# Two layers with recurrent mixers on one core: the second part of 59 weight units by an accumulating transfer within SBUF

## The chip, the cores and the metric

The kernel runs on one core of a Trainium2 chip. The metric is the device time of one launch in microseconds (us). TensorE (PE) multiplies, VectorE (DVE), ScalarE (ACT) and GpSimd (POOL) work on elements, and transfers are issued from the queue of SyncE (SP) or of POOL and are carried out by 16 DMA engines. PE keeps a queue for loading weights of its own (PEld).

## The reference

A prompt of 512 tokens and 8 samples of one token each go through two layers of width 1024. The first layer joins a gated linear recurrence (RG-LRU) and a state-space scan (SSD), the second is a gated linear attention with 16 heads (HGRN2). Each layer ends with a gated embedding. All is float32.

```python
def layer_ab(h, p, ...):
    u = rmsnorm(h, norm_w) @ w_in
    a_x, a_gate, b_z, b_xbc, b_dt = jnp.split(u, ...)
    ...                                   # convolutions, RG-LRU, SSD
    mix = jnp.concatenate([a_out, b_out], axis=-1).astype(h.dtype) @ w_out
    h = h + mix
    h = per_layer_embed(h, p, ple_w, ple_g)

def layer_c(h, p, ...):
    u = rmsnorm(h, norm_w) @ w_in
    q, fx, v, gate = jnp.split(u, [HK_C, 2 * HK_C, 2 * HK_C + D_C], axis=-1)
    ...                                   # chunks of 128 tokens, 16 heads
    h = h + o.astype(h.dtype) @ w_out
    h = per_layer_embed(h, p, ple_w, ple_g)

def per_layer_embed(h, p, w_proj, w_gate):
    gate = jax.nn.sigmoid((h @ w_gate).astype(F32))
    return h + (gate * (p @ w_proj).astype(F32)).astype(h.dtype)
```

## The kernel before

Tokens lie along the free axis (520 = 512 + 8), features on partitions. A projection is computed in tiles of 128 output features. For float32 accuracy each weight and each activation is split into two parts of type float32r (`hi`, the rounded value, and `lo`, the rest), and three of the four products are added: `whi` by `xh`, `whi` by `xl`, `wlo` by `xh`, each for two halves of 260 tokens. A *unit* is a block of weights of 128 partitions x 1024 elements (512 KB), mostly 8 blocks of 128 rows by 128 columns; it makes 48 products.

Units are read in program order: `ax` (the recurrence's input), `xbc` (12 units), `z` and `ag` (gates, 8 units each), `oa` and `ob` (output), `pg` (the embedding's gate), and in layer 1 for each pair of heads two units each of `f`, `v`, `q`, `g`, and at times four of the output `o`. `section` lists them in *groups* of two neighbouring units, which `load_group` brings in by one transfer of 1 MB on SP's queue into one of two buffers `wraw` (128 x 2048). `split_unit` copies a unit to `whi` (on ACT or DVE) and subtracts: `wlo` = `wraw` - `whi` on DVE. Two buffers each of `whi` and `wlo` feed PE.

```python
            copy(hv, v)
            tt(lv, v, hv.bitcast(F32), SUB, eng)
```

All instructions are first recorded by `Plan` and then put in an order: with an estimate of each cost, an engine that comes free takes the recorded instruction of the earliest place in the program whose operands are there. `side(...)` moves the place of what is recorded in it; `SPLIT_AHEAD` and `LOAD_AHEAD` say how many us of the main stream ahead of a unit its splitting and its loading stand. The order found so is fixed: each engine and each queue runs its own list in order and waits at the first entry that is not ready. All instructions are issued by one line (L510), so the profile is read by the names of tiles.

Beside the projections stand: the small products on POOL that make `dtt` (the step sizes of the SSD, through `htmp`), on which the product `acs` of PE waits; `wsl`, the SSD's weights; `smp`, the samples' states of the SSD (512 KB in and out); `l1c` and `l1d`, the same in layer 1; `pl`, the embedding, kept in DRAM (`pl_d`) until its gate is there.

Of the kernel before, what the change touches and what calls it, by code (L numbers as in the profile page):

```python
# [42 lines left out]
# how far ahead of a unit its weights are split and loaded, in us of the main stream  # L43
SPLIT_AHEAD, LOAD_AHEAD = 1.67, 11.54
# how far ahead of the main stream goes what it waits for, in us
MARGIN = 38.78
# an engine waits for an instruction that is more urgent by URGENT us, up to this part of the time of the one at hand
# [32 lines left out]
def _mm(n, a, k):  # L80
    out, m = k["out"] if "out" in k else a[0], k["lhsT"].shape[-1]
    if m < 128 and out.off >= 32 * ROW:
        # beside the one before it, in other columns of the array
        return 65 if k["rhs"].dtype == F32R else 125
    return max(n, 256) if k["rhs"].dtype == F32R else 4 * max(n, m)
# [17 lines left out]
class Buf:  # L103
    """A tile that is allocated when its first instruction is issued."""
# [7 lines left out]
class View:  # L112
    """A view of a Buf; offset and strides are in elements, a partition is ROW apart."""
# [86 lines left out]
class Op:  # L200
    """One instruction, in a form for each engine that may take it, or a few matrix products that stay together."""
# [8 lines left out]
class Plan:  # L210
    """Instructions are collected first and then put in an order: with an estimate of what each of them costs, an
    engine that comes free takes the instruction of the earliest place in the program whose operands are there."""
# [6 lines left out]
    # -- collecting --  # L219
# [22 lines left out]
    @contextmanager  # L242
    def side(self, start=0.0, rate=0.0, pinned=False):
        """Instructions whose place is moved, by a start and by their own time so far; pinned: for good."""
        keep = self.shift, self.rate, self.pinned
        self.shift, self.rate, self.pinned = start, rate, pinned
        yield
        self.shift, self.rate, self.pinned = keep

    @contextmanager  # L250
    def together(self, *views):
        """Instructions that wait until all of some operands are written."""
        self.gate = self.barrier([o for v in views for box, o, w in v.buf.acc if w and _meet(box, v.box())])
        yield
        self.gate = None

    @contextmanager
    def block(self, main=False):
        """Matrix products that stay together."""
# [66 lines left out]
    # -- ordering --  # L326
    def hold_banks(self):
        """A PSUM bank is taken only when what its readers wait for otherwise is already on its way."""
# [7 lines left out]
    def urgency(self):  # L336
        """What an instruction of the main stream waits for is put ahead of it."""
# [10 lines left out]
    def order(self):  # L348
# [44 lines left out]
        def pick(e, t):  # L393
            """The instruction for engine e at time t, or when there may be one."""
# [7 lines left out]
            while av:  # L402
# [13 lines left out]
                if func and table not in IN_SET[func]:  # L416
                    # another table: first what the loaded one can do, for a while
# [14 lines left out]
            if got:  # L432
                heapq.heappush(av, got)
                hold = {"dve": HOLD_DVE, "act": HOLD_ACT, "pool": HOLD_POOL}.get(e)
                if hold:
                    # rather wait a little for one that is more urgent than be in its way
# [8 lines left out]
        while left:  # L445
# [27 lines left out]
            else:  # L473
                if e == "pe":
                    # the clock is halved after a window with too few columns
# [17 lines left out]
    # -- issuing --  # L493
# [27 lines left out]
# the place of the side work: its start after the instructions it follows, and its pace  # L521
# [9 lines left out]
def hybrid_decode_step_kernel(ctx: ExitStack, tc: tile.TileContext, I, O, mode="both"):  # L531
# [31 lines left out]
    def grab(name):  # L563
        """One of four PSUM banks for the side work; it is given back by its last reader."""
        return new("psa", [128, 512], "ax", name)
# [25 lines left out]
    def copy(out, in_):  # L591
        """A copy on either engine."""
        plans[-1].record(("act", "copy", (out, in_), {}), ("dve", "tensor_copy", (out, in_), {}))

    def scaled(out, in_, s):
        """in_ times a column, on either engine."""
# [10 lines left out]
    groups, units, sec = [], [], {}  # L607

    def section(name, ap, k0, kk, c0, ncols, uc, per=2):
        sec[name] = len(units)  # L610
        for c in range(c0, c0 + ncols, per * uc):
            w = min(per * uc, c0 + ncols - c)
            groups.append((ap, k0, kk, c, w))
            for s in range(0, w, uc):
                units.append((len(groups) - 1, s, uc, kk))

    raw_of, split_of = {}, {}

    def load_group(g):
        ap, k0, kk, c, w = groups[g]  # L620
        r = new("wp", [128, 2048], "raw", f"wraw{g}", 2)
        v = r[:, :kk * w].rearrange("p (k c) -> p k c", k=kk)
        with side(*((plans[-1].shift, 0.0, True) if plans[-1].pinned else (-LOAD_AHEAD,))):
            sp.dma_start(out=v, in_=ap[k0 * 128:(k0 + kk) * 128, c:c + w].rearrange("(k p) c -> p k c", p=128))
        raw_of[g] = v

    def split_unit(u, hi=None, lo=None, eng=dve):
        g, s, uc, kk = units[u]
        if g not in raw_of:
            load_group(g)  # L630
        v = raw_of[g][:, :, s:s + uc]
        if hi is None:
            hi = new("wp", [128, 1024], "whi", f"whi{u}", 2, F32R)
            lo = new("wp", [128, 1024], "wlo", f"wlo{u}", 2, F32R)
        hv = hi[:, :kk * uc].rearrange("p (k c) -> p k c", k=kk)
        lv = lo[:, :kk * uc].rearrange("p (k c) -> p k c", k=kk)
        with side(*((plans[-1].shift, 0.0, True) if plans[-1].pinned else (-SPLIT_AHEAD,))):
            copy(hv, v)
            tt(lv, v, hv.bitcast(F32), SUB, eng)
# [5 lines left out]
    section("ax", w_in0, 0, 8, 0, 256, 128, 1)  # L645
    section("ax2", w_in0, 0, 8, 256, 768, 128)
    section("proj0", I["ple_proj"][0], 0, 2, 0, 512, 256, 1)
    section("proj0b", I["ple_proj"][0], 0, 2, 512, 512, 512, 1)
# [30 lines left out]
    pair_sections("r", "fgvq")  # L679
    K8 = list(range(8))  # L680

    def project_both(tiles, pair, kmap):
        """One or two tiles of 128 output features (column block m of unit u) over all tokens."""
# [28 lines left out]
    def split_p(pk, ps8, pp, layer):  # L712
        """p with features on partitions, in two float32r parts."""
# [23 lines left out]
    for i in range(2):  # L737
        with side(-69.0, pinned=True):
            load_group(units[sec["proj0"] + i][0])
        with side(-67.0 + i * W1, pinned=True):  # L740
            split_unit(sec["proj0"] + i)
    with side(-65.0, pinned=True):
        for i in range(4):
            if i == 1:
                load_group(units[sec["proj0b"]][0])
# [17 lines left out]
    # the tensor engine's clock rises only under load: products of constants until the first tokens are there  # L763
# [43 lines left out]
    def rsqrt_mean(dst, src, n, width):  # L807
        """(src / n + eps) ** -0.5 on a few columns."""
# [8 lines left out]
    def scale_split(src, w, R, xh, xl, name):  # L817
        """src times its weight and a row of factors per token, in two float32r parts."""
# [6 lines left out]
    # the tokens with features on partitions; they come back as the residual  # L825
# [94 lines left out]
    def log1p_of(z, n, lo):  # L920
        """log(1+z) for z in [0,1], from the odd series in z/(2+z)."""
# [14 lines left out]
    def accurate_exp(t, k):  # L936
        """exp in place: the table on x/2^k, where it is exact to float32, and k squarings."""
# [4 lines left out]
    def buffers():  # L942
        """Samples: convolution buffers and LRU state with features on partitions."""
# [11 lines left out]
    def tables():  # L955
        pool.memset(triu, 1.0)
        select(triu, [[1, 128]], 0, -1, 0.0)
        # RG-LRU: -8 softplus(-lam), halved for the sigmoid from tanh
# [10 lines left out]
        # the convolution on x/B/C is halved: silu(2 y) = y (1 + tanh(y))  # L969
# [9 lines left out]
    def lower_bounds():  # L979
        """The lower bound of layer 1 is the second of two softmax rows."""  # L980
# [10 lines left out]
        # is every lower bound large enough for one reference per chunk of layer 1?  # L991
# [6 lines left out]
        # if not, the fast way runs on bounds that keep it finite, and its results are replaced  # L998
# [5 lines left out]
        # with sigmoid(x) = (1 + t) / 2, t = tanh(x / 2): k = cneg (t - 1), decay = ch t + fb  # L1004
# [10 lines left out]
    # the first weights have a place of their own  # L1015
# [41 lines left out]
    def gates(j):  # L1057
        """r and i as tanh of the halved argument; 1 - a^2 = (1 + a^2) tanh(-log a)."""
# [37 lines left out]
    def lru(j0):  # L1096
        """The recurrence over the prompt and one step of the samples."""
# [70 lines left out]
    def dt_project():  # L1168
        """dt with heads on partitions, the parts of its weights side by side, then with tokens there; the fifth
        block ends with the samples."""  # L1170
# [85 lines left out]
    def ssd_chunk(g, c):  # L1256
# [11 lines left out]
        # exp(acs_t - acs_s) for s <= t  # L1268
# [17 lines left out]
        # features on partitions: two heads side by side  # L1286
# [44 lines left out]
    def smp_start(g):  # L1331
        """B and C of the samples on every partition, by way of DRAM."""
# [771 lines left out]
```

## Time and profile before

| | before |
|---|---|
| time, median of 3 runs | 1078.1 us (1075.42 to 1078.21) |
| span of the profiled execution | 1075.0 us |
| its own time | not listed apart; the three runs are 0.4 to 3.2 us above the span |
| busy PE, DVE, ACT, POOL | 1044.0, 778.2, 509.1, 144.6 us |
| bytes moved by DMA | 138.43 MB, 129 GB/s over the span |

The page gives busy time by engine, then groups of instructions (name of the output, names of the inputs, partitions x elements, count, busy us, mean ns of one, idle time of the engine before them and what ended it). A wait names the waiting instruction first, then what released it. A row of a stretch gives start and end, the stretch's length, the busy time of each engine, the granted clock of PE, the mean busy share of the 16 DMA engines and GB/s.

### The profile page before, as it was taken

How to read it: one execution, taken by the hardware profiler on the slowest of the kernel's cores; microseconds unless marked ns; L12 is line 12 of the kernel's file. 1: busy time of each engine (PE TensorE's matmuls, PEld its weight loads, DVE VectorE, ACT ScalarE, POOL GpSimd, SP SyncE). 2: the span in 40 equal slices, each digit the busy share in tenths (PEclk: the TensorE clock that was granted, in tenths of full speed). 3: DMA queues.
4: the chain of work that ended last, by engine and by line, in shares of the span. 5: the costliest groups of instructions: out<-in, count | busy, mean ns of one | idle time of the engine just before them, and what ended most of it. 6: DMA issues, size and time to landing. Idle time of an engine off the chain costs nothing.

```text
span 1075.0 us, 21235 instructions
## 1 busy us (share of the span) xinstructions
PE 1044.0 (97%) x8595; PEld 1023.0 (95%) x8595; DVE 778.2 (72%) x1521; ACT 509.1 (47%) x1196; POOL 144.6 (13%) x247
## 2 busy tenths in 40 slices
PE   9899989999999999999999999999999999999995
PEld 8899988899999999999999999999999999999995
DVE  6879988999997546774858576675765757667753
ACT  6476648636464212353445545333463344642453
POOL 3755475200000000100000000000000000000000
PEclk9899999999999999999999999999999999999998
DMA  8603226444686233563433433253342433335311
GB/s 275 244 21 99 80 51 206 147 142 140 200 249 210 79 115 131 162 208 88 135 108 115 128 102 111 90 155 91 115 124 87 143 98 112 97 89 199 119 40 44
DMA packets 130466, 138.43 MB, mean 129 GB/s; under 512 B 13704, under 2 KB 111128, under 8 KB 130344
## 3 DMA queue, kind: packets, MB, share of 16 engines
q1 hardware_dynamic: 130136, 136.93, 41.0%
q8 instruction: 69, 1.13, 0.4%
q14 instruction: 37, 0.30, 0.1%
q0 software_dynamic: 224, 0.06, 0.0%
HBM read 111.71 MB, written 25.44 MB: 128 GB/s over the span
## 4 chain that ended last, share of the span: by engine, by line
PE 84%; POOL 5%; DVE 4%; DMA 3%; ACT 2%; issue 1%; POOLq 0%; ACTq 0%; DVEq 0%
PE o L510 11%; PE g L510 10%; PE f L510 9%; PE v L510 9%; PE q L510 9%; PE pg L510 7%; PE ag L510 4%; PE ob L510 4%; PE z L510 4%; PE oa L510 3%; PE ax L510 3%; PE xbc L510 1%; POOL csm L510 1%; PE A L510 1%; PE kv L510 1%
## 5 line engine op out<-in xcount | busy, mean ns | idle before, releaser
L510 DVE TENSOR_TENSOR wlo<-wraw,whi 128x1024 fp32r<-128x1024 f32 (+1 forms) x143 | 173.4, 1213 | 3.2 <-ACT whi L510 1.8
L510 ACT CAST whi<-wraw 128x1024 fp32r<-128x1024 f32 (+1 forms) x63 | 65.2, 1036 | 126.3 <-PE q L510 41.2
L510 POOL TENSOR_TENSOR at__1873<-at__1873,nhalf 128x4 f32<-128x4 f32 (+1 forms) x24 | 20.8, 866 | 501.1 <-DVE at__1873 L510 501.1
L510 DVE CAST whi<-wraw 128x1024 fp32r<-128x1024 f32 x80 | 55.3, 692 | 36.7 <-PE v L510 11.9
L510 PE MATMUL g<-xh,whi 128*128 128x260 f32 x256 | 55.8, 299 | 0.0
L510 PE MATMUL q<-xh,whi 128*128 128x260 f32 x256 | 53.2, 289 | 0.0
L510 PE MATMUL o<-oh,whi 128*128 128x260 f32 x256 | 52.6, 286 | 0.0
L510 PE MATMUL v<-xh,whi 128*128 128x260 f32 x256 | 52.1, 285 | 0.0
L510 PE MATMUL v<-xh,wlo 128*128 128x260 f32 x256 | 51.5, 283 | 0.0
L510 PE MATMUL g<-xl,whi 128*128 128x260 f32 x256 | 51.5, 283 | 0.0
L510 PE MATMUL o<-oh,wlo 128*128 128x260 f32 x256 | 51.5, 283 | 0.0
L510 PE MATMUL g<-xh,wlo 128*128 128x260 f32 x256 | 51.5, 283 | 0.0
L510 PE MATMUL o<-ol,whi 128*128 128x260 f32 x256 | 51.4, 282 | 0.0
L510 PE MATMUL q<-xl,whi 128*128 128x260 f32 x256 | 51.4, 282 | 0.0
L510 PE MATMUL v<-xl,whi 128*128 128x260 f32 x256 | 51.4, 282 | 0.0
L510 PE MATMUL q<-xh,wlo 128*128 128x260 f32 x256 | 51.4, 282 | 0.0
L510 PE MATMUL f<-xh,whi 128*128 128x260 f32 x240 | 50.6, 292 | 0.0
L510 PE MATMUL f<-xl,whi 128*128 128x260 f32 x240 | 48.2, 282 | 0.0
L510 PE MATMUL f<-xh,wlo 128*128 128x260 f32 x240 | 48.2, 282 | 0.0
L510 DVE SCALAR_TENSOR_TENSOR l1a<-q,lbt,l1a 128x260 f32<-128x260 f32 (+1 forms) x32 | 14.0, 479 | 44.1 <-PE q L510 44.0
L510 DVE SCALAR_TENSOR_TENSOR l1c<-l1d,l1c 128x128 f32<-128x128 f32 x128 | 40.9, 345 | 0.6 <-ACT l1c L510 0.6
L510 PEld LDWEIGHTS o<-oh,whi 128*128 128x128 f32 x256 | 39.3, 189 | 0.9 <-issue 0.8
(507 smaller groups left out, 3362.2 us busy)
## 6 DMA issues: line engine op xcount, KB each, us to landing
wraw<-in_c_w_in_dram SPq DMA_DIRECT2D x32, 1024.0 KB
wraw<-in_ab_w_in_dram SPq DMA_DIRECT2D x15, 1024.0 KB
wraw<-in_ab_w_out_dram SPq DMA_DIRECT2D x8, 1024.0 KB
wraw<-in_ple_gate_dram SPq DMA_DIRECT2D x8, 1024.0 KB
l1c<-in_state_c_dram SPq DMA_DIRECT2D x16, 512.0 KB
out_dram<-l1c SPq DMA_DIRECT2D x16, 512.0 KB
wraw<-in_c_w_out_dram SPq DMA_DIRECT2D x8, 1024.0 KB
pl<-pl_d SPq DMA_DIRECT2D x2, 2080.0 KB
```

Source lines behind the costliest of these rows:

```text
L510: getattr(f, name)(*a, **k)
```

## The change

Units are loaded one at a time, 512 KB each, into two buffers `wraw` of half the size; the space goes to a third buffer each of `whi` and `wlo`. For the units in `by_dma` (the 28 of `xbc`, `z` and `ag`, and in layer 1 the second unit of each `f`, `v`, `q`, `g`, except the first pair's `f`: 31) the second part is made otherwise: `whi` is copied, `wlo` is set to its negative on ACT or DVE, and a transfer issued by POOL adds `wraw` to `wlo` (both in SBUF, 128 rows of 4 KB). These three stand `HI_AHEAD` = 11.0 us ahead, loads 15.0 instead of 11.54. The embedding `pl` is read back in eight pieces instead of one transfer, in both layers. Comments are dropped; all other constants stay.

```diff
-SPLIT_AHEAD, LOAD_AHEAD = 1.67, 11.54
+SPLIT_AHEAD, LOAD_AHEAD, HI_AHEAD = 1.67, 15.0, 11.0
...
-def load_group(g):
-        ap, k0, kk, c, w = groups[g]
-        r = new("wp", [128, 2048], "raw", f"wraw{g}", 2)
...
+    def wtile(tag, u, bufs, dt=F32R):
+        _, kk, uc = units[u]
+        return new("wp", [128, 1024], tag, f"{tag}{u}", bufs, dt)[:, :kk * uc].rearrange("p (k c) -> p k c", k=kk)
...
+    def load_raw(u):
+        raw_of[u] = wtile("wraw", u, 2, F32)
+        with ahead(LOAD_AHEAD):
+            sp.dma_start(out=raw_of[u], in_=units[u][0])
...
-        with side(*((plans[-1].shift, 0.0, True) if plans[-1].pinned else (-SPLIT_AHEAD,))):
-            copy(hv, v)
-            tt(lv, v, hv.bitcast(F32), SUB, eng)
+        rv = raw_of[u]
+        if u not in by_dma:
+            with ahead(SPLIT_AHEAD):
+                copy(hv, rv)
+                tt(lv, rv, hv.bitcast(F32), SUB, eng)
+        else:
+            with ahead(HI_AHEAD):
+                copy(hv, rv)
+                scaled(lv, hv.bitcast(F32), -1.0)
+                pool.dma_start(out=lv, in_=rv, accum_op=ADD)
...
+    by_dma.update(range(sec["xbc"], sec["out0a"]))
+    by_dma.update(sec[f"{nm}{pr}"] + 1 for nm in "fvqg" for pr in range(8) if nm + str(pr) != "f0")
...
-    sp.dma_start(out=pl0, in_=pl_d[0].rearrange("k p n -> p k n"))
+    for j in range(8):
+        with side(2.67 * j):
+            sp.dma_start(out=pl0[:, j], in_=pl_d[0][j])
...
-        with side(-20.0):
-            sp.dma_start(out=pl1, in_=pl_d[1].rearrange("k p n -> p k n"))
+        for j in range(8):
+            with side(-12.0 + 2.67 * j):
+                sp.dma_start(out=pl1[:, j], in_=pl_d[1][j])
```

How the lists change at the places of which the prediction speaks. First SP's queue late in layer 0, where PE works on `ag` and then on the last four `z`; before it reads:

```order
L510 DMA wraw_3042<-in_ab_w_in_dram 128x8x256
L510 DMA smp<-in_state_b_ssm_dram 128x8x128
L510 DMA out_dram<-wsl 128x4x128
L510 DMA wraw_3226<-in_ab_w_in_dram 128x8x256
L510 DMA out_dram<-smp 128x8x128
L510 DMA smp<-in_state_b_ssm_dram 128x8x128
```

and of the changed kernel:

```order
L510 DMA wraw_3083<-in_ab_w_in_dram 128x8x128
L510 DMA out_dram<-smp 128x8x128
L510 DMA out_dram<-wsl 128x4x128
L510 DMA wraw_3206<-in_ab_w_in_dram 128x8x128
L510 DMA smp<-in_state_b_ssm_dram 128x8x128
L510 DMA out_dram<-smp 128x8x128
L510 DMA wraw_3295<-in_ab_w_in_dram 128x8x128
```

Loads have half the columns and stand twice as often between the states; each waits for the buffer of the unit two before it.

Second POOL's list in `xbc`, where `dtt` is made through `htmp` (`xa` and `LCb` belong to the recurrence and the convolution). Before:

```order
L510 TENSOR_SCALAR dtt<-dtt 128x80
L510 TENSOR_SCALAR htmp<-dtt 128x80
L510 TENSOR_TENSOR xa<-lr,AH_507 128x8
L510 TENSOR_TENSOR htmp<-dtt,htmp 128x80
L510 COPY LCb<-bcs 128x11
```

and of the changed kernel:

```order
L510 COPY LCb<-bcs 128x11
L510 TENSOR_SCALAR dtt<-dtt 128x80
L510 DMA wlo_1669<-wraw_1544 128x1024
L510 TENSOR_SCALAR htmp<-dtt 128x80
L510 TENSOR_TENSOR htmp<-dtt,htmp 128x80
```

The issue of an accumulating transfer stands between two steps of the chain; two more follow further down, ahead of its end. On PE the product `acs`, which waits for this chain, stands 12 products later in `xbc` than before.

Third ACT's list late in layer 0, where `sga` is the first step on a finished unit of `ag`. Before:

```order
L510 ACTIVATE sga_3270<-ag_3178 128x520
L510 CAST whi_3278<-wraw_3042 128x1024
L510 ACTIVATE prod,ysm<-prod 128x128 x8
L510 ACTIVATE sga_3345<-ag_3263 128x520
L510 ACTIVATE smp<-smp,sfm 128x128 x8
```

and of the changed kernel:

```order
L510 ACTIVATE sga_3439<-ag_3358 128x520
L510 ACTIVATE wlo_3450<-whi_3441 128x1024
L510 ACTIVATE sga_3499<-ag_3432 128x520
L510 ACTIVATE wlo_3510<-whi_3501 128x1024
L510 ACTIVATE sga_3563<-ag_3492 128x520
L510 ACTIVATE wlo_3574<-whi_3565 128x1024
```

A negation now follows each `sga`, so it cannot go before PE has finished the unit three before its own.

More of the change, by code (lines that the diff above doesn't have):

```diff
@@ L604, in ltile, with section @@
         return new("lay", shape, name, name, dt=dt)
-    groups, units, sec = [], [], {}
-    def section(name, ap, k0, kk, c0, ncols, uc, per=2):
+    units, sec = [], {}
+    def section(name, ap, k0, kk, c0, ncols, uc):
         sec[name] = len(units)
[L611 to L615, printed above, removed]
@@ L617, in hybrid_decode_step_kernel @@
-    raw_of, split_of = {}, {}
-    def load_group(g):
-        ap, k0, kk, c, w = groups[g]
-        r = new("wp", [128, 2048], "raw", f"wraw{g}", 2)
[L622 to L625, printed above, removed]
-    def split_unit(u, hi=None, lo=None, eng=dve):
[L628 to L636, printed above, removed]
-        with side(*((plans[-1].shift, 0.0, True) if plans[-1].pinned else (-SPLIT_AHEAD,))):
-            copy(hv, v)
-            tt(lv, v, hv.bitcast(F32), SUB, eng)
+        for c in range(c0, c0 + ncols, uc):
+            units.append((ap[k0 * 128:(k0 + kk) * 128, c:c + uc].rearrange("(k p) c -> p k c", p=128), kk, uc))
@@ new lines, in hybrid_decode_step_kernel, with ahead @@
+    raw_of, split_of, by_dma = {}, {}, set()
+    def wtile(tag, u, bufs, dt=F32R):
+        _, kk, uc = units[u]
+        return new("wp", [128, 1024], tag, f"{tag}{u}", bufs, dt)[:, :kk * uc].rearrange("p (k c) -> p k c", k=kk)
+    def ahead(us):
+        return side(*((plans[-1].shift, 0.0, True) if plans[-1].pinned else (-us,)))
+    def load_raw(u):
+        raw_of[u] = wtile("wraw", u, 2, F32)
+        with ahead(LOAD_AHEAD):
+            sp.dma_start(out=raw_of[u], in_=units[u][0])
+    def split_unit(u, hi=None, lo=None, eng=dve):
+        ap, kk, uc = units[u]
+        if u not in raw_of:
+            load_raw(u)
+        hv, lv = (wtile(nm, u, 3) if t is None else t[:, :kk * uc].rearrange("p (k c) -> p k c", k=kk)
+                  for nm, t in (("whi", hi), ("wlo", lo)))
+        rv = raw_of[u]
[8 more added lines that the diff above has]
+                pool.dma_start(out=lv, in_=rv, accum_op=ADD)
@@ L644, in hybrid_decode_step_kernel @@
     XBC = [8, 10, 0, 1, 2, 3, 4, 5, 6, 7, 9, 11]
-    section("ax", w_in0, 0, 8, 0, 256, 128, 1)
+    section("ax", w_in0, 0, 8, 0, 256, 128)
     section("ax2", w_in0, 0, 8, 256, 768, 128)
-    section("proj0", I["ple_proj"][0], 0, 2, 0, 512, 256, 1)
-    section("proj0b", I["ple_proj"][0], 0, 2, 512, 512, 512, 1)
+    section("proj0", I["ple_proj"][0], 0, 2, 0, 512, 256)
+    section("proj0b", I["ple_proj"][0], 0, 2, 512, 512, 512)
     section("xbc", w_in0, 0, 8, 3072 + 1024, 128, 128)
@@ L738, in hybrid_decode_step_kernel @@
         with side(-69.0, pinned=True):
-            load_group(units[sec["proj0"] + i][0])
+            load_raw(sec["proj0"] + i)
         with side(-67.0 + i * W1, pinned=True):
@@ L744, in hybrid_decode_step_kernel @@
             if i == 1:
-                load_group(units[sec["proj0b"]][0])
+                load_raw(sec["proj0b"])
             if i == 2:
```

## The prediction

> **What bounds the kernel now.** I read the page first (busy time, groups), then the chain of waits, then the waits of PE, then busy time by stretch, then single transfers on the queues.
>
> ```profile
> span 1075.0 us, 21235 instructions
> PE 1044.0 (97%) x8595; PEld 1023.0 (95%) x8595; DVE 778.2 (72%) x1521; ACT 509.1 (47%) x1196; POOL 144.6 (13%) x247
> L510 DVE TENSOR_TENSOR wlo<-wraw,whi 128x1024 fp32r<-128x1024 f32 (+1 forms) x143 | 173.4, 1213 | 3.2 <-ACT whi L510 1.8
> L510 ACT CAST whi<-wraw 128x1024 fp32r<-128x1024 f32 (+1 forms) x63 | 65.2, 1036 | 126.3 <-PE q L510 41.2
> L510 DVE CAST whi<-wraw 128x1024 fp32r<-128x1024 f32 x80 | 55.3, 692 | 36.7 <-PE v L510 11.9
> ```
>
> PE is busy for all but 31 us, so DVE work that goes away is worth at most what PE idles on its account. The stretches (busy us of PE, PEld, DVE, ACT, POOL, then granted clock, DMA share, GB/s) say where the 31 us lie:
>
> ```profile
> 0.00:60.00 60.00, 52.09 (x359) 49.05 (x360) 39.66 (x74) 28.82 (x58) 36.07 (x83) 0.94 0.70 233
> 140.00:150.00 10.00, 5.80 (x42) 5.41 (x42) 5.16 (x9) 3.58 (x10) 8.60 (x21) 0.91 0.19 52
> 160.00:170.00 10.00, 9.85 (x82) 9.64 (x81) 10.00 (x16) 8.18 (x17) 3.71 (x5) 1.00 1.09 360
> 180.00:200.00 20.00, 17.58 (x145) 15.21 (x144) 19.04 (x33) 16.57 (x45) 8.15 (x17) 1.00 0.23 80
> 255.70:302.70 47.00, 47.00 (x394) 46.98 (x393) 43.24 (x89) 28.09 (x117) 0.00 (x0) 1.00 0.67 208
> 460.00:1000.00 540.00, 539.87 (x4496) 532.66 (x4497) 367.73 (x805) 242.36 (x572) 20.77 (x24) 1.00 0.39 117
> 1060.00:1075.00 15.00, 2.98 (x25) 2.52 (x23) 3.57 (x10) 3.55 (x8) 1.65 (x3) 0.71 0.22 78
> ```
>
> Of the 31 us, 7.9 lie in the first 60 us and 12.0 in the last 15, where no unit of this change is split. Layer 1 (460 to 1000) has 0.13 us. What DVE could give back lies between 140 and 200: 4.2 + 0.15 + 2.4 us. The waits of PE name those:
>
> ```profile
> PE acs L510 <- POOL dtt L510: 4.2, 1, 4.2
> PE yd L510 <- DVE wsl L510: 1.8, 1, 1.8
> ```
>
> The first is a chain on POOL, not on DVE. So the prize is small, and the question is whether the new chain of a unit (load, copy, negate, transfer) keeps up with PE. PE's pace, from the chain (start, us, what) and from the rows of wlo:
>
> ```profile
> 255.71 22.36 PE ag L510 x186
> ...
> 576.48 6.67 PE f L510 x54
> ...
> 633.37 6.67 PE f L510 x54
> L510 PE MATMUL xbc<-xnh,wlo x192: 277/282/420, 96.9 to 178.8; 128*128 128x260 f32 x192
> ```
>
> A unit is 48 products: 22.36 x 48 / 186 = 5.77 us where nothing stands between (255 to 303, called dense below). Twelve xbc units take 81.9 us, 6.83 each. A pair of heads in layer 1 takes 633.37 - 576.48 = 56.9 us with 8 units, 7.11 each. Two units, which is how long a raw buffer of two may be held, are 11.5, 13.7 and 14.2 us.
>
> **The change, part by part.** *DVE and ACT.* 59 subtractions leave DVE: 59 x 1.213 = 71.6 us. The order puts 39 negations on ACT and 20 on DVE; they are passes over one operand of the size of the copies, so 39 x 1.036 = 40.4 us on ACT and 20 x 0.692 = 13.8 us on DVE. ACT is half idle and PE covers both; the negation counts only as a step of the chain of a unit.
>
> *Loads.* The prices of a transfer come from three that stand alone on the queues (issue, then the stretch in which they move):
>
> ```profile
> 84.81 0.37 SPq L510 DMA_DIRECT2D wraw<-in_ab_w_in_dram  x1
> 85.00:88.20 3.20, 3.20 (x27) 3.05 (x26) 2.72 (x11) 0.64 (x2) 0.52 (x1) 1.00 0.62 169
> 90.31 8.75 SPq L510 DMA_DIRECT2D wraw<-in_ab_w_in_dram  x2
> 91.00:95.00 4.00, 4.00 (x35) 4.00 (x35) 3.64 (x8) 3.92 (x8) 0.88 (x2) 1.00 0.80 262
> 222.81 0.32 SPq L510 DMA_DIRECT2D acy<-acsT_d  x1
> 223.50:226.00 2.50, 2.50 (x24) 2.50 (x23) 2.50 (x8) 0.20 (x1) 0.00 (x0) 1.00 0.64 210
> ```
>
> The first is one unit, 512 KB in rows of 512 B: 0.62 x 3.2 = 2.0 us of all engines, landed 3.4 us after its issue. The second is a group of two units in rows of 1 KB: 0.80 x 4.0 = 3.2 us, landed 4.7 us after. Two single loads so cost 0.8 us more of the engines than a group, up to 72 x 0.8 = 58 us in all, 5% of the span. This lies beside PE (DMA share 0.39 in layer 1) and costs nothing by itself; without that cover it costs room in the dense stretch, below. The third has 4 KB rows, as the new transfer: 0.64 x 2.5 = 1.6 us, landed 3.2 us after the issue.
>
> *The accumulating transfer.* No row shows one. It reads its destination too, so its engine time lies between 1.6 us (as a plain copy) and 3.2 (twice that); 59 are 94 to 189 us, 9 to 18% of the span. It is issued by POOL, and small transfers of that queue show what its fixed part may be (KB, us from issue to landing), and its issue:
>
> ```profile
> prow<-in_a_conv_w_dram POOLq DMA_DIRECT2D x1, 16.0 KB, 4.0
> prow<-in_a_lam_dram POOLq DMA_DIRECT2D x1, 4.0 KB, 6.2
> 1.56 0.81 POOL L510 DMA_DIRECT2D prow<-in_a_conv_w_dram  x1
> 4.92 0.54 POOL L510 DMA_DIRECT2D prow<-in_b_conv_b_dram  x1
> ```
>
> Both were taken with DMA near full. The bounds from issue to landing are 3.2 us (the plain copy) and 6.2 + 3.2 = 9.4. I take 4.0 + 1.6 = 5.6 where DMA is half idle and 4.0 + 3.2 = 7.2 in the dense stretch, since the lowest row of the same queue is nearest and the share there (0.67) leaves no room: 31.5 us of 47 are used, 8 single loads add 3, 8 accumulations add 13 to 26, together 47 to 60.
>
> By the Trainium skill, Collectives: The Full Stack, section Part 3 (The bandwidth ceiling), a reduction by DMA runs at half the rate of a copy, because each result takes two reads; its figures are 32.35 against 62.28 GB/s. By that rule landing is 7.2 us in layer 1 too, and the sum below would be 5 us higher, about 1092; no run here shows it yet.
>
> *How long a raw buffer is held.* Load 3.4, copy 0.9 (the mean of both engines), negation 1.0, transfer 5.6 or 7.2, and 1.0 for four hand-overs to engines that are in the middle of something: 11.9 or 13.5 us. The next unit of that buffer cannot be loaded before.
>
> - Dense: 13.5 - 11.5 = 2.0 us late per round of two units, four rounds, 8.0. The three buffers of whi and wlo allow a unit's copy two units ahead, so the first lands 11.5 - 0.9 - 1.0 - 7.2 - 0.5 = 1.9 us early. Cost 6 us; 0 at a landing of 5.6, 17 at 9.4.
> - xbc and z: 13.5 against 13.7, even; where the queue is full (share 1.09 at 160 to 170) a round or two is late. Cost 2; 0 to 6.
> - Layer 1, where every other unit is one of these: 11.9 against 14.2. Once in each pair the load goes out behind the states:
>
> ```profile
> 518.00:534.00 16.00, 16.00 (x130) 15.13 (x129) 12.26 (x35) 5.99 (x17) 1.58 (x2) 1.00 0.61 176
> 532.55 24.44 SPq L510 DMA_DIRECT2D wraw<-in_c_w_in_dram  x3
> 534.00:539.00 5.00, 5.00 (x44) 5.00 (x44) 4.18 (x9) 3.02 (x5) 0.00 (x0) 1.00 0.98 208
> ```
>
>   The load issued at 532.55 moves until 539, 6.5 us against 4.7 alone, so that round has 13.7 (hidden) or, at a landing of 7.2, 15.3: 1.1 late, 7 pairs, 8 us. I take 3, nearer to the lower end as the share is half. At 9.4 all 31 units are late by 15.7 - 14.2: 46 us.
>
> *POOL.* Three issues stand inside the chain of small products that ends in dtt, for which PE waits 4.2 us. Behind each waits that chain; they cost 3 x 0.54 to 0.81 = 1.6 to 2.4 us. PE has 12 more products ahead of acs, 1.4 us. Net 0.5; 0 to 2, more if an issue waits long for its negation.
>
> *What DVE's relief gives.* At 180 to 200 DVE is busy 19.0 of 20 us and PE waits 1.8 for wsl: gain 2; between 0 and all of 4.2 + 2.4 = 6.6. The loads of pl in eight pieces and the first loads move nothing that PE waits for: 0 (-1 to 1).
>
> Sum: 6 + 2 + 3 + 0.5 - 2 = 9.5 us. The profiled execution has a span of 1075.0; the runs shown go from 1075.4 to 1078.2, so 0.4 to 3.2 us lie around it. I add to the median, 1078.1, 3.1 above the span: 1087.6, say 1087.
>
> **The rivals.** *Hidden anyway.* If a landing takes 5.6 us everywhere, dense rounds are 11.9 against 11.5 with 1.9 and more to spare: nothing is late, 0.5 - 2 remain: 1077. For it: the plain copy's 3.2 us and the free half of DMA in layer 1. Against: the POOL rows, none below 4.0.
>
> *Faster.* Operations of DVE make those of POOL slower; the chain to dtt shows it with one product while DVE still works and the same while it idles (it is busy 5.16 of the 10 us from 140):
>
> ```profile
> 138.94 1.05 POOL L510 TENSOR_TENSOR htmp<-htmp 128x80 f32<-128x80 f32 x1
> 144.40 0.35 POOL L510 TENSOR_TENSOR htmp<-htmp 128x80 f32<-128x80 f32 x1
> ```
>
> With less on DVE that chain (some 15 us) shortens by up to a quarter and both waits vanish: 1078.1 - 6.6 = 1071.5. It decides if landings stay below about 6 us and the three issues fit into POOL's gaps.
>
> *Starved issues.* The same rows read the other way: what POOL does takes 1.05 / 0.35 = 3 times as long beside DVE, which is busy 43.24 of the dense 47 us. An issue of 0.81 that takes 2.4 makes a landing of 8.8: dense 4 x (15.1 - 11.5) - 0 = 14, xbc and z 10 rounds x 1.4 = 14, layer 1 31 x (15.1 - 14.2) = 28, and 0.5 - 2: 1132. It decides from 8 us on, where every round of layer 1 is late. By the Trainium skill, SBUF — State Buffer, section SBUF: two separate sides, this is a rule: a DMA issued by GpSimd waits for its descriptors while DVE runs a two-port operation such as a float32 copy (620 ns become 3100). The slowed rows agree in kind; no run here shows it for an issue. Against it as the likeliest: DVE's copies of that sort are 0.69 us long and few.
>
> **How the numbers follow.** A measurement of this kernel can tell about 0.3%, 3.2 us, from no change. Forecast (a few late rounds, 1082 to 1112): 0.46. Hidden, within 3.2 us of 1078.1: 0.25. Faster: 0.17. Starved or otherwise above 1112: 0.12. Slower is 0.46 + 0.12 = 0.58. The range 1072 to 1112 leaves out the starved case and about half of the faster one, 0.20. Within the forecast alone it would be 1082 to 1112.
>
> **What would show it.** DVE's group of wlo falls to 84 products, near 102 us; a new ACT group has 39, near 40 us; DVE about 58 us less busy. POOL's queue moves about 31 MB. PE's own waits get a new line, a product of ag or z on the transfer into wlo, of 1 to 2 us each, dense stretch first; the wait on acs stays near 4. Landing in the DMA list near 5.6, over 7 in the dense stretch. Wrong if the landing is below 5 (then hidden or faster) or above 8 (then layer 1 is slow all through), or if the idle time is on other waits than wlo.

## The result, and the profile after

The changed kernel takes 1101.2 us (median of 4 runs, 1099.14 to 1103.35), the kernel before beside it 1077.96 (1075.42 to 1078.21). These medians part by 23.2 us, a ratio of 1.0216. The ratio estimated for this comparison is a little higher, 1.0237 with a 95% interval of 1.0218 to 1.0257, which is 25.5 us; where ratios are set against each other below, it is this one. The profiled execution has a span of 1097.4 us, 22.4 longer than before.

The page of the changed kernel, its rows that answer to those of before (busy time by engine; the queue of POOL with packets, MB and share of 16 engines; the groups around the second part; the transfer's median time to landing):

```profile
span 1097.4 us, 21611 instructions
PE 1050.9 (96%) x8595; PEld 1028.8 (94%) x8595; DVE 749.2 (68%) x1538; ACT 526.4 (48%) x1179; POOL 191.4 (17%) x306
q0 software_dynamic: 8720, 31.00, 14.6%
L510 POOL DMA_DIRECT2D wlo<-wraw x59 | 52.9, 896 | 455.9 <-ACT wlo L510 248.5
L510 DVE TENSOR_TENSOR wlo<-wraw,whi 128x1024 fp32r<-128x1024 f32 (+1 forms) x84 | 101.4, 1207 | 5.9 <-DMA out_dram<-in_state_b_conv_dram 3.1
L510 ACT ACTIVATE wlo<-whi 128x1024 fp32r<-128x1024 f32 x39 | 41.3, 1058 | 24.5 <-DVE whi L510 24.2
wlo<-wraw POOLq DMA_DIRECT2D x59, 512.0 KB, 4.9
```

DVE lost its 59 subtractions and has time to spare, and yet PE idles longer: 1097.4 - 1050.9 = 46.5 us against 31.0. That is 15.5 of the 22.4 us. The other 6.9 are in PE's busy time: the same 8595 products take 1050.9 us instead of 1044.0, at a lower granted clock in some places, which are shown below. PE's own waits, and the products that mark the stages:

```profile
PE yd L510 <- DVE wsl L510: 6.5, 2, 4.1
PE acs L510 <- POOL dtt L510: 6.2, 1, 6.2
PE z L510 <- DVE sga L510: 2.9, 1, 2.9
PE q L510 <- DMA wlo<-wraw: 1.2, 1, 1.2
L510 PE MATMUL xbc<-xnh,wlo x192: 277/282/420, 96.3 to 191.5; 128*128 128x260 f32 x192
L510 PE MATMUL z<-xnh,wlo x128: 277/282/420, 192.1 to 320.2; 128*128 128x260 f32 x128
L510 PE MATMUL f<-xh,wlo x240: 277/282/291, 481.8 to 940.0; 128*128 128x260 f32 x120
```

Only 1.2 us in all are waits of PE on the new transfer itself. PE waits for small work: `wsl`, `dtt`, `sga`. The twelve `xbc` units take 95.2 us (81.9 before), `z` and `ag` 128.1 (123.0), and layer 1 begins 18.1 us late (463.7 before). So most of the loss is in layer 0. Against the kernel before, the larger part of that is in `xbc`; the run without transfers, below, corrects this.

What a gap does to the clock, read from short stretches of `xbc` (length, PE's busy time, granted clock, DMA share, GB/s):

```profile
144.00:148.00 4.00, 2.19 (x19) 1.00 0.45 129
148.00:150.00 2.00, 0.00 (x0) 0.81 0.07 14
150.00:152.00 2.00, 0.00 (x0) 0.50 1.08 215
153.00:156.00 3.00, 3.00 (x16) 0.50 0.48 105
156.00:160.00 4.00, 4.00 (x35) 0.99 1.04 231
```

PE waits 6.2 us for `dtt`, and the three busy us behind it hold 16 products instead of some 25 (the dense pace before, 394 in 47 us). In layer 0 the same follows four more times: behind the waits of 4.1 and 2.4 us for `wsl`, of 2.9 for `sga`, and of 0.9 and 1.3 us in close succession for `oa`. Two of these stretches of the changed kernel, then the one stretch of the kernel before, behind its wait of 4.2 us:

```profile
188.00:190.00 2.00, 2.00 (x10) 0.50 0.82 162
302.00:304.00 2.00, 2.00 (x12) 0.50 0.97 299
```

```profile
150.00:152.00 2.00, 2.00 (x13) 0.60 0.08 17
```

So these waits are paid again in part at half clock: between 96 and 340 us five times now and once before.

Behind those small waits the chain of waits shows what is late (start, us, what):

```profile
115.64 4.42 DMA wlo<-wraw
120.12 6.67 DMA wraw<-in_ab_w_in_dram
153.11 7.94 DMA wlo<-wraw
161.07 7.51 DMA wraw<-in_ab_w_in_dram
206.27 8.47 DMA acy<-acsT_d
240.22 4.71 DMA smp<-in_state_b_ssm_dram
264.92 6.15 DMA wlo<-wraw
271.08 7.18 DMA wraw<-in_ab_w_in_dram
```

A unit's load, 3.4 us alone before, takes 6.7 to 7.5 us in these rows (3.6 and 3.9 in two others of the chain), and `acy`, a scratch transfer of 512 KB, takes 8.5; before, one of its kind took 3.2 us alone and another 6.4 where the engines were full, at 160. DMA is 13% of this chain, against 3% before. Two theories fit these rows: buffers held until landings (the prediction's), or the 16 engines shared with the new traffic.

### The profile page after: what moved, and what is told of

Same layout as the page of the kernel before. It is cut to its first block, busy times and chain, and to the rows that moved or that the text cites. A ratio compares the mean times of both kernels' runs of the same rounds, so it can differ in the third digit from the quotient of the medians.

```text
span 1097.4 us, 21611 instructions
## 1 busy us (share of the span) xinstructions
PE 1050.9 (96%) x8595; PEld 1028.8 (94%) x8595; DVE 749.2 (68%) x1538; ACT 526.4 (48%) x1179; POOL 191.4 (17%) x306
## 4 chain that ended last, share of the span: by engine, by line
PE 71%; DMA 13%; DVE 6%; POOL 3%; ACT 3%; issue 2%; SPq 0%; POOLq 0%; DVEq 0%; ACTq 0%
PE o L510 11%; PE pg L510 8%; PE q L510 8%; PE g L510 8%; PE f L510 8%; PE v L510 7%; DMA wlo<-wraw 4%; PE oa L510 4%; PE ob L510 4%; PE ax L510 3%; DMA wraw<-in_ab_w_in_dram 3%; PE pl L510 2%; DMA x_d<-xT 2%; POOL htmp L510 1%; DMA wraw<-in_c_w_in_dram 1%
## 5 line engine op out<-in xcount | busy, mean ns | idle before, releaser
L510 ACT CAST whi<-wraw 128x1024 fp32r<-128x1024 f32 (+1 forms) x65 | 67.4, 1037 | 148.4 <-PE ob L510 37.0
L510 POOL DMA_DIRECT2D wlo<-wraw x59 | 52.9, 896 | 455.9 <-ACT wlo L510 248.5
L510 DVE TENSOR_TENSOR wlo<-wraw,whi 128x1024 fp32r<-128x1024 f32 (+1 forms) x84 | 101.4, 1207 | 5.9 <-DMA out_dram<-in_state_b_conv_dram 3.1
L510 DVE CAST whi<-wraw 128x1024 fp32r<-128x1024 f32 x78 | 53.9, 691 | 70.3 <-DMA wraw<-in_c_w_in_dram 30.5
L510 PE MATMUL g<-xh,whi 128*128 128x260 f32 x256 | 55.8, 299 | 0.0
L510 PE MATMUL q<-xh,whi 128*128 128x260 f32 x256 | 53.1, 289 | 0.0
L510 ACT ACTIVATE wlo<-whi 128x1024 fp32r<-128x1024 f32 x39 | 41.3, 1058 | 24.5 <-DVE whi L510 24.2
L510 PE MATMUL o<-oh,whi 128*128 128x260 f32 x256 | 52.8, 287 | 0.0
L510 PE MATMUL q<-xh,wlo 128*128 128x260 f32 x256 | 51.6, 283 | 1.2 <-DMA wlo<-wraw 1.2
L510 PE MATMUL v<-xh,whi 128*128 128x260 f32 x256 | 52.1, 285 | 0.0
L510 PE MATMUL v<-xh,wlo 128*128 128x260 f32 x256 | 51.5, 283 | 0.0
L510 PE MATMUL g<-xl,whi 128*128 128x260 f32 x256 | 51.5, 283 | 0.0
L510 PE MATMUL o<-oh,wlo 128*128 128x260 f32 x256 | 51.5, 283 | 0.0
L510 PE MATMUL v<-xl,whi 128*128 128x260 f32 x256 | 51.5, 283 | 0.0
L510 PE MATMUL g<-xh,wlo 128*128 128x260 f32 x256 | 51.5, 282 | 0.0
L510 PE MATMUL o<-ol,whi 128*128 128x260 f32 x256 | 51.4, 283 | 0.0
L510 PE MATMUL q<-xl,whi 128*128 128x260 f32 x256 | 51.4, 282 | 0.0
L510 PE MATMUL f<-xh,whi 128*128 128x260 f32 x240 | 50.5, 291 | 0.0
L510 PE MATMUL f<-xl,whi 128*128 128x260 f32 x240 | 48.2, 282 | 0.0
L510 PE MATMUL f<-xh,wlo 128*128 128x260 f32 x240 | 48.2, 282 | 0.0
L510 POOL TENSOR_TENSOR at__1931<-at__1931,nhalf 128x4 f32<-128x4 f32 (+1 forms) x24 | 25.6, 1067 | 102.5 <-DVE at__1931 L510 102.5
L510 DVE SCALAR_TENSOR_TENSOR l1a<-q,lbt,l1a 128x260 f32<-128x260 f32 (+1 forms) x32 | 14.0, 480 | 42.1 <-PE q L510 42.1
```

The lines of the kernel that those rows point to most:

```text
L510: getattr(f, name)(*a, **k)
```

## Experiments

All ratios are against the kernel before, run on the same chip beside each group of runs. Three theories stood at the start: 1, raw buffers held until the landing delay the next loads; 2, POOL's list, in which the issues delay the small products and the chain to `dtt`; 3, the single loads and the new order.

**What of the change costs nothing.** First the changed kernel with the set of transferred units empty, and with the transfers in layer 1 alone.

```diff
-    by_dma.update(range(sec["xbc"], sec["out0a"]))
-    by_dma.update(sec[f"{nm}{pr}"] + 1 for nm in "fvqg" for pr in range(8) if nm + str(pr) != "f0")
```

> No unit by transfer: single loads, three buffers of whi and wlo, all subtractions on DVE; a new order. Theories 1 and 2: 1074 to 1082, as before the change. Theory 3: 1094 to 1101.

1076.75 us, ratio 1.0010 (0.9998 to 1.0021). Single loads, the third buffers and `pl` in pieces cost nothing.

With only the first of the two lines taken away:

> Only the 31 units of layer 1 by transfer. The traces of before and after part by 18 us before layer 1 and by 4 in it. Theories 1 and 2: 1079 to 1084. Theory 3: 1094 to 1101.

1080.7 us, ratio 1.0044 (1.0029 to 1.0059): 4.7 us for 31 units. The 28 units of layer 0 make the other 18 to 21.

**Held buffers.** The transfer takes `whi` as its source in place of `wraw`, so that the raw piece is free after the copy (the second part becomes zero); and, apart from that, a third raw buffer for the changed kernel (for its room some small tiles share a place; those lines are left out here).

```diff
                 pool.dma_start(out=lv, in_=rv, accum_op=ADD)
+                plans[-1].ops[-1].forms["pool"][0][0][2]["in_"] = hv.bitcast(F32)
```

> The changed kernel with every list of every engine as it is; the 59 transfers add whi instead of wraw (so the second part is left out, it becomes zero). Then a raw buffer is free after the copy and not held until the transfer has landed. Held buffers (theory 1): loads no longer wait for landings, the waits of DVE and ACT on wraw (51 and 33 us or more in the changed kernel) nearly vanish, 1080 to 1085 us. POOL's list (theory 2: the issues delay the small products and the chain to dtt): nothing changes for POOL, 1097 to 1101. Single loads and the new order (theory 3): 1097 to 1101.

1099.65 us, ratio 1.0210 (1.0151 to 1.0269).

```diff
-                    b.real = self.pools[b.pool].tile(..., bufs=b.bufs)
+                    b.real = self.pools[b.pool].tile(..., bufs=3 if b.tag == "wraw" else b.bufs)
```

> The changed kernel with its lists as they are, but with a third raw buffer (room from two small tiles that share a place with others). Theory 1: three units are 20.5 us of PE in xbc, a buffer is held 14 to 18 us, so most lateness goes: 1080 to 1087. Theories 2 and 3: 1097 to 1101.

1100.8 us, ratio 1.0232 (1.0197 to 1.0266). The rows of `z` and `f`, first of the run with the raw piece freed, then of that with three buffers:

```profile
L510 PE MATMUL z<-xnh,wlo x128: 277/282/291, 194.5 to 316.4; 128*128 128x260 f32 x128
L510 PE MATMUL f<-xh,wlo x240: 277/282/291, 475.7 to 940.1; 128*128 128x260 f32 x120
```

```profile
L510 PE MATMUL z<-xnh,wlo x128: 277/282/291, 198.1 to 318.8; 128*128 128x260 f32 x128
L510 PE MATMUL f<-xh,wlo x240: 277/282/291, 477.6 to 941.9; 128*128 128x260 f32 x120
```

Here the hold is seen, and seen to be small: `z` and `ag` take 121.9 and 120.7 us instead of 128.1. How the hold reaches PE is seen in the changed kernel: DVE stands at the copy of a raw piece that was loaded late, and the `sga` that PE needs comes behind it in DVE's list.

```profile
298.99 0.69 DVE L510 CAST whi<-wraw 128x1024 fp32r<-128x1024 f32 x1 [8.39 <-DMA wraw<-in_ab_w_in_dram]
300.34 0.80 PE L510 MATMUL z<-xnh,whi 128*128 128x260 f32 x2 [2.94 <-DVE sga L510]
```

With the raw piece freed, DVE waits 5.8 us for raw pieces between 92 and 330 instead of 20.4, and this wait of PE is gone. But `xbc` takes as long as in the changed kernel or longer (it ends at 193.9 and 197.5), and layer 1 loses what was won: from the first to the last product of `f` it takes 464.4 and 464.3 us instead of 458.2, and there PE now waits 7.0 and 6.1 us on the transfer itself. Held buffers fall as the main cause.

**Movement, POOL's list or the order** (theories A, B and C of the expectations). One element per partition instead of 1024; no transfer at all; and all transfers but those of `xbc`.

```diff
-                k = {x: v.resolve() ... for x, v in k.items()}
+                k = {x: (v[:, 0, 0:1] if "accum_op" in k else v).resolve() ... for x, v in k.items()}
```

> The lists of all engines are those of the changed kernel; each of the 59 accumulating transfers moves one element of each partition (128 x 4 bytes) in place of 128 x 4 KB, so GpSimd still issues it at the same place and behind the same negation, but almost nothing is moved. Left out: the rest of the second part stays the negative of the first. Theory A, the movement itself (landing 4.9 us in the middle, up to 11.5, and loads that take 6.7 to 7.5 us beside it in place of about 3.4): most of the loss goes, 1080 us (1076 to 1085), xbc takes about 85 us, as without transfers, in place of 95. Theory B, GpSimd's list (an issue of 0.9 us that waits for its negation, with the chains to dtt and the scans' small operands behind it): the loss stays, 1097 us (1092 to 1102), the wait for dtt stays near 6 us. Theory C, the order of the lists on ScalarE and VectorE, with 59 negations in front of small work: it stays too, 1097 us.

1080.3 us, ratio 1.0048 (1.0031 to 1.0064).

```diff
-                getattr(f, name)(*a, **k)
+                None if k.get("accum_op") else getattr(f, name)(*a, **k)
```

> The changed kernel's lists without the 59 transfers: the raw piece is free after its copy, the second part is the negative of the first, and GpSimd's list is shorter by 59 issues; the copies and negations on VectorE and ScalarE stand where they stood. Left out: the raw piece is never added. Theory A: 1079 us (1075 to 1084), as with the tiny transfers. Theory B: 1079 us as well, but clearly below the run with tiny transfers, by 12 us or more. Theory C: 1096 us (1091 to 1101), as with them; dtt is waited for 6 us as before.

1076.1 us, ratio 1.0004 (0.9992 to 1.0017). PE's wait for `dtt`, with tiny transfers and then without any:

```profile
PE acs L510 <- POOL dtt L510: 6.2, 1, 6.2
```

```profile
PE acs L510 <- POOL dtt L510: 4.7, 1, 4.7
```

Theory A holds for the larger part: 18 to 20 us go with the movement. B holds for a part that I had priced at half a us: 59 issues, their places in POOL's list and the landings of the tiny transfers (2.0 us in the middle) together cost 4 to 5 us (1080.3 against 1076.1), some 1.5 of it in the direct wait for `dtt`. C falls: the new order with all negations costs nothing. The last run also tells what the idea could win at best. It has the subtractions off DVE, the negations in their place and no transfers, and is as fast as before: on balance DVE's relief is worth nothing here.

By the rows of this run `xbc` takes 88.1 us and `z` with `ag` 118.0: the order alone moves 5 to 6 us from the one to the other. Against it the changed kernel loses 7.1 us in `xbc` and 10.1 in `z` and `ag`.

The direct reading is the same scratch transfer `acy` at the same place. First the changed kernel, then tiny transfers (start, us, engine, instruction, in brackets the wait before it and what ended it):

```profile
204.44 0.87 POOL L510 DMA_DIRECT2D wlo<-wraw  x1 [4.98 <-ACT wsl L510]
206.27 0.32 SPq L510 DMA_DIRECT2D acy<-acsT_d  x1
214.89 1.60 POOL L510 TENSOR_SCALAR_AFFINE_SELECT wsl<-acy 128x1024 f32<-128x1024 f32 x1 [4.27 <-DMA acy<-acsT_d]
```

```profile
202.38 0.87 POOL L510 DMA_DIRECT2D wlo<-wraw  x1 [5.00 <-ACT wsl L510]
204.19 0.32 SPq L510 DMA_DIRECT2D acy<-acsT_d  x1
210.13 1.09 POOL L510 TENSOR_SCALAR_AFFINE_SELECT wsl<-acy 128x1024 f32<-128x1024 f32 x1 [1.60 <-ACT wsl L510]
```

Issued 1.8 us behind the accumulating transfer, `acy` lands after 8.47 us (the chain above) and POOL waits for it; behind the tiny one it has landed by the time POOL asks, 5.9 us after its issue at the latest.

```diff
-    by_dma.update(range(sec["xbc"], sec["out0a"]))
+    by_dma.update(range(sec["z"], sec["out0a"]))
```

> The transfers are kept for the 16 units from z on in layer 0 and the 31 of layer 1; the 12 xbc units are subtracted on VectorE, loads are single ones, and the lists are planned anew. If most of layer 0's loss arises in xbc (95 us there against 85 without any transfer), by whatever mechanism: 1089 us (1084 to 1093). If the loss is a toll of each transfer (23 us / 59 = 0.39 us each), 47 of 59 remain: 1096 us (1094 to 1099).

1092.8 us, ratio 1.0167 (1.0123 to 1.0211): the median lies at the upper end of the first expectation and the interval reaches over the second, so it does not tell them apart. It does place the loss, to some 5 us: with layer 1's 4.7 us taken off, the 16 units of `z` and `ag` cost about 13 us, the twelve of `xbc` the remaining 7 or 8. That agrees with the rows just given. It is the run in which PE waits longest on the transfer itself:

```profile
PE z L510 <- DMA wlo<-wraw: 7.9, 3, 5.0
```

With the units of `xbc` subtracted, PE comes to `z` sooner, and there the second parts are late at the product.

**Traffic or late landings.** Same transfers, but added to a scratch tile that nobody reads, from the negated second part:

```diff
+    def aside(self, k):
+        ...
+        return dict(k, out=self.pools["dum"]..., in_=k["out"].bitcast(F32))
...
+                k = self.aside(k) if "accum_op" in k else k
```

> The changed kernel's lists, and transfers of the same size (512 KB, 4 KB rows, accumulating) at the same places, but each adds the negated second part to a scratch tile that nobody reads; the product takes the second part as soon as the negation is done, and the raw piece is free after its copy. Left out: the raw piece is never added. So the traffic stays and nobody on TensorE's path waits for a landing (only the second part's own buffer is held until then). Traffic theory (the transfers make the loads and the small DMAs beside them slow): 1097 us (1092 to 1102), loads beside transfers still take 6 to 8 us. Landing theory (the second part is late at the product): 1081 us (1077 to 1086), as with one element per partition (1080.3).

1095.9 us, ratio 1.0198 (1.0158 to 1.0239). This speaks for traffic, with a flaw: each transfer waits for the landing of the one before it in the scratch tile (the added lines make L510 into L518 here).

```profile
POOL dum L518 <- DMA dum<-wlo: 31.5, 6, 6.5
```

These are POOL's waits between 92 and 330 us; the price of that new wait is mixed in. Next, plain copies of the same 512 KB, and accumulating transfers of half the columns:

```diff
-                getattr(f, name)(*a, **k)
+                getattr(f, name)(*a, **{x: v for x, v in k.items() if x != "accum_op"})
```

> The changed kernel with the same lists and the same transfers, but plain copies within SBUF in place of accumulating ones (the second part becomes the whole weight; left out: the addition). If a transfer within SBUF costs the same whether it adds or not: 1100 us (1096 to 1103). If the reading back and adding makes the transfer dear (2.7 us of the engines and 4.9 us to landing, against 1.6 and 3.2 us of a plain load of 512 KB in 4 KB rows): 5 us of list and 18 us of movement x 1.6 / 2.7 give 1091 us (1086 to 1094), or down to 1081 if only the long landings hurt.

1080.4 us, ratio 1.0062 (1.0035 to 1.0089).

```diff
+                k = {x: (v[:, 0:v.shape[1] // 2] if "accum_op" in k else v).resolve() ...
```

> The changed kernel with the same lists, each transfer only over the first half of its columns (256 KB, 2 KB rows; left out: the addition in the other half). If the loss goes with the bytes: half way between 1080.3 (one element) and 1101: 1090 us (1087 to 1094). If it has a threshold, because a landing of about 3.5 us is still in time: 1083 us (1080 to 1086).

1084.0 us, ratio 1.0101 (1.0084 to 1.0118). POOL's queue and the landings, of plain copies and of half transfers:

```profile
q0 software_dynamic: 8720, 31.00, 8.2%
L510 POOL DMA_DIRECT2D wlo<-wraw x59 | 33.9, 575 | 451.7 <-ACT wlo L510 242.9
wlo<-wraw POOLq DMA_DIRECT2D x59, 512.0 KB, 3.0
```

```profile
q0 software_dynamic: 8720, 15.53, 8.1%
wlo<-wraw POOLq DMA_DIRECT2D x59, 256.0 KB, 3.3
```

Both came out where the expectations had put late landings (1081 and 1083), so up to here that theory was not beaten. A plain copy of 512 KB and an accumulating one of 256 KB take the same time of the engines, 0.082 x 1080 / 59 = 1.5 us each, and cost 1.5 and 5.7 us more than the tiny transfer; the full accumulating ones, at 2.7 us each, cost 20 more. So the loss does not go with the bytes, and the first half of the engine time is cheap while the second is not. Why the two at 1.5 us differ by some 4 us stays open; the plain copy is also issued faster (0.575 us against 0.88).

**All waits taken away at once.** Turned round, the transfer adds the negated second part into the raw piece, with two raw buffers and with three:

```diff
+                k = dict(k, out=k["in_"], in_=k["out"].bitcast(F32)) if "accum_op" in k else k; ...
```

> The changed kernel's lists on all engines, with two raw buffers. Each transfer of 512 KB is turned round: it adds the negated second part into the raw piece, which nobody reads after the copy. So the traffic, GpSimd's issues and the raw buffer's hold until the landing stay, but the product takes the second part as soon as it is negated, and GpSimd waits for no landing. Left out: the second part never gets the raw piece. If the late landing at the product is the loss: 1083 us (1078 to 1088). If traffic or hold makes it: 1098 us (1093 to 1102). This has no scratch tile, whose own landing GpSimd had to wait for, 31.5 us in six waits.

1111.9 us, ratio 1.0317 (1.0238 to 1.0395), dearer than expected by either theory. Why it is worse than the changed kernel stays open.

> As the run with transfers turned round into the raw piece, and with a third raw buffer besides: neither the product nor the next load waits for a landing in the usual case; only the traffic and GpSimd's 59 issues are left. Left out: the second part never gets the raw piece. If the traffic alone makes the loss: 1096 us (1091 to 1101). If landing and hold make it together, so that taking away one of them (the runs with the raw buffer freed early, with three raw buffers) shows little: 1082 us (1078 to 1087), as with tiny transfers.

1095.0 us, ratio 1.0186 (1.0144 to 1.0228). Traffic again, though SP's queue still waits for the raw buffers there. So the last pair takes away nearly every wait for a landing: the source is `whi`, and the third product of these units reads `whi` too.

```diff
+                plans[-1].ops[-1].forms["pool"][0][0][2]["in_"] = hv.bitcast(F32); lv.buf.twin = hv.buf
...
+                k = {x: (View(v.buf.twin, ...) if x == "lhsT" and hasattr(v.buf, "twin") else v).resolve() ...
```

> The changed kernel's lists. Each accumulating transfer of 512 KB adds whi into wlo, so the raw piece is free after its copy, and the third product of these 59 units takes whi in place of wlo, so that TensorE waits for no landing; no scratch tile, so GpSimd waits for none either. Left out: the second part. Every earlier run left one such wait in place; here only the traffic and the 59 issues are left. If the traffic on the 16 engines by itself makes loads and small transfers late: 1094 us (1089 to 1100). If each time the one wait that was left made the loss: 1081 us (1077 to 1085), as with one element per partition.

1093.8 us, ratio 1.0180 (1.0149 to 1.0211). The same with plain copies:

> As the run in which nobody waits for a landing, but with plain copies of the same 512 KB (1.5 us of the engines in place of 2.7). Left out: the second part and the addition. If what counts is the time that the transfers take on the engines: 1080 us (1077 to 1084), however the run with accumulating ones comes out. If bytes count: as that run, 1094 us.

1080.0 us, ratio 1.0043 (1.0021 to 1.0065).

The medians differ by 14 us (9 to 20 by the ends of the two intervals). Besides the time that the same 31 MB take on the engines, only POOL's issue differs, 0.87 us against 0.57 in the middle. That it is not the issue is told by the tiny transfers, which are issued as slowly (0.90) and stand at 1.0048. Of waits for a landing the accumulating run keeps two, 4.8 us of DVE and 2.0 of ACT, both in layer 1, which takes the same time in both runs (455.2 and 454.9 us from the first to the last product of `f`). The dense stretch from 260 to 300, first of the accumulating run, then of the plain one, with the chain's DMA rows of the first between them (its profiled execution is the fastest of its four, 1084.9 us, so it shows less than the median):

```profile
260.00:300.00 40.00, 40.00 (x335) 1.00 1.02 252
```

```profile
166.26 10.83 DMA wraw<-in_ab_w_in_dram
288.31 4.33 DMA sb_d<-acsT
292.65 5.78 DMA smp<-sb_d
302.35 7.32 DMA wraw<-in_ab_w_out_dram
```

```profile
260.00:300.00 40.00, 40.00 (x335) 1.00 0.83 259
```

At about the same GB/s (252 and 259) the engines are full in one (share 1.02) and have room in the other (0.83). PE itself is busy through both; the 6.6 us between the two profiled spans (1083.0 and 1076.4) are waits of PE elsewhere, 5.0 of them for `wsl`, `aol` and `aoh`, small work of DVE and ACT. One cause is seen at 166, where the engines are full too: the load issued at 166.26 lands after 10.83 us and DVE waits for it, while in the plain run the load at the same place, issued at 165.81, has landed when DVE takes it at 175.16, after 9.4 us at the latest. POOL waits there 3.1 us for `acy`, against 0.7. So with the engines full, loads and scratch transfers land late although PE waits for no new transfer, and some of what PE needs of POOL, DVE and ACT comes late with them.

## Why the prediction was right or wrong

The sign was right, and so was the description of the change. The size was not: 9 us were forecast, 23 came. The 1101.2 us lie inside the range given, 1072 to 1112, but its upper part was there for landings of up to 9.4 us that hold buffers, and landings of 4.9 us came; that the time fell inside is luck. The signs of being wrong did appear, a landing below 5 and idle time on other waits than `wlo`, but what I had tied to the first, hidden or faster, did not follow.

- **Instructions.** DVE's group has 84 subtractions and 101.4 us (forecast 102), ACT's negations 39 and 41.3 (40), POOL's queue 31.00 MB (31). DVE is 29.0 us less busy, not 58, and ACT 17.3 more, not 40: by the counts, 58 instructions that either engine can take moved from ACT to DVE.
- **The transfer's price.** Forecast 1.6 to 3.2 us of the engines, measured 0.146 x 1097.4 / 59 = 2.7; landing forecast 5.6 and 7.2, measured 4.9 in the middle. With the tiny transfer's 0.013 x 1078.4 / 59 = 0.24 us taken off as fixed, adding costs (2.72 - 0.24) / (1.50 - 0.24) = 1.96 times a plain copy. By the Trainium skill, Collectives: The Full Stack, Part 3 (The bandwidth ceiling), a reduction by DMA in a collective runs at half the rate of a copy; the traces here agree, for an addition within SBUF. The 1092 us that I worked out beside it are still too low: I let the rule act only on the unit's own landing (7.2 us by it, 4.9 measured).
- **Dense, +6.** The hold was right in size: 6.2 and 7.4 us of `z` and `ag` go when the raw piece is freed or tripled. Its way to PE was not the one forecast: PE waits for no `wlo` there, but for `sga`, which stands behind a late raw piece in DVE's list, and then runs at half clock. It did not decide the end: those runs are at 1.0210 and 1.0232, since in layer 1 PE then waits on the transfer.
- **The new transfers beside all others, 0.** This is the step that failed. In the sum the engine time of the 59 (94 to 189 us) acted only through the landing and the hold of their own units. I had worked out that the dense stretch is full (47 to 60 us of engine time in 47) and had seen a load slowed to 6.5 us by the states beside it, but what full engines do to the loads and scratch transfers of others stood at nothing. The words "costs nothing by itself" were said of the single loads, and for these they held (1.0010); I never asked the same of the accumulations. The runs show in its place some 14 us: the accumulating run in which PE waits for no landing is that much slower than the plain one.
- **xbc and z, +2 (0 to 6).** Too small: 7.1 us in `xbc` and, beside the hold, some 3 in `z` and `ag`, against the same order without transfers. I had looked for weight rounds that come late, not for `acy`, `smp` and the single loads' own landings.
- **Layer 1, +3 (0 to 8).** Right in size, 4.7 us alone. The rounds late behind the states, from which I had it, are not shown: in the changed kernel PE waits there 2.1 us for `l1a` and 1.2 on the transfer.
- **POOL, +0.5 (0 to 2).** Too small: 4 to 5 us with tiny transfers over none.
- **DVE's relief, -2.** Nothing: 1.0004 without transfers. The rival *faster* falls with it: the slowed POOL operations were no prize, `dtt` is still waited for 4.7 us.
- **Starved issues.** An issue takes 0.90 us in the mean (0.85 to 1.30), against 0.81 assumed and 2.4 feared. The issue times show nothing of the stall that the Trainium skill, SBUF — State Buffer, states for such a DMA, and tiny transfers land in 2.0 us in the middle.
- **Clock.** Not in the sum at all: 6.9 of the 22.4 us. The Trainium skill, TensorE: Matmul & The Clock Gate, Part 1, has the clock halved after an idle window of about 3.4 us; the 0.50 behind the wait of 6.2 us agrees, but here waits of 2.4 and 2.9 us had it too, and the measurement decides.

How the loss divides, from runs whose intervals leave each part open by several us: issues and POOL's list 5, engines filled by the accumulation 14, holds and late landings the rest, 4 to 6. What of the 14 comes through loads and what through scratch transfers was not separated.

## What to carry to other kernels

Before moving work from an engine to DMA, price what it does to every other transfer that is under way: add the engine time of the new one to the share of the stretch, and where the sum nears 1, expect late landings there, of transfers that have nothing to do with the new one too; here loads of 3.4 us took up to 7.5 and `acy` 8.5. Before that, take the work away entirely in a trial: here the subtractions were worth nothing, and PE's waits on DVE before, 1.8 us for `wsl`, had left little to win. And count a wait of PE with what it costs in clock: behind waits of 2.4 to 6.2 us some 3 to 6 us of its products ran at half clock.

## What the runs showed of the hardware

An accumulating transfer within SBUF (512 KB, 4 KB rows) takes 2.7 us of the 16 engines and lands in 4.9 us in the middle (4.6 to 5.7 in its variants), a plain copy through the same queue 1.5 and 3.0 (4.3 with `whi` as its source), an accumulating one of 4 bytes per partition 0.24. POOL takes 0.90 us to issue the accumulating one, and 0.88 and 0.90 for half of it and for one element, but 0.575 for the plain copy. The step between cheap and dear was sharper than I had expected: with 1.5 us of the engines each, the 59 transfers add 0 to 6 us to the time with tiny ones; with 2.7 us each they add 14 to 20, and 29 where they were turned round into two raw buffers.
